# Token sums by column halves, gate products on VectorE, weight sums from tile 11.5, query rows ahead of the gathers

## The chip, the cores and the metric

The kernel runs on one core of a Trainium2 chip. Its engines have their own instruction streams: TensorE (PE) multiplies matrices, VectorE (DVE) and ScalarE (ACT) work elementwise, GpSimd (POOL) does some elementwise work and issues DMA transfers, SyncE (SP) issues most of the transfers. An engine executes its stream in order and waits where an operand isn't there yet. The metric is the device time of one launch in microseconds, as a median of several runs; a profile is one further execution.

## What is computed

One step of a decoder layer, for a prompt of 1024 tokens and 8 sample tokens (1032 columns in all, width 2048). The core of it:

```python
h = rmsnorm(x, norm_w)
(aq, ak, av, iq, ik, iw, az, mq, mk, mv, mi, mf, mo, mz) = split(h @ w_in)
# attention group: an indexer scores all keys, the best 256 are attended to
s     = relu(einsum('bqhd,bld->bqlh', iq, ik))
_, idx = top_k(einsum('bqlh,bqh->bql', s, iw) * IDX_SCALE, 256)
att   = softmax(q @ k[idx] * ATT_SCALE) @ v[idx]
# mLSTM group: chunks of 64 tokens with a carried matrix state C, n, m
h_ml  = mlstm_run(mq, mk, mv, mi, mf)
a     = att * silu(az)
m     = rmsnorm_heads(h_ml) * ml_norm_w * sigmoid(mo) * silu(mz)
y     = rmsnorm(x + concat([a, m]) @ w_out, final_norm_w)
```

For the sample tokens the keys and values are gathered from a paged cache of 4096 past positions, and the mLSTM continues from a given state. Besides `y` the kernel returns the new keys, values, index keys and mLSTM states.

## The kernel before

Everything is float32. A product of two float32 matrices is made of three matmuls of a rounded high part and a low part (`xH`, `xL` for the tokens, `wH`, `wL` for the weights): ACT casts the high part, DVE subtracts it to get the low part.

The input projection runs in 61 tiles of 128 output columns. `proj` (L1500 for its matmuls) makes tile 0 (index keys, indexer weights, gates), tiles 1 to 8 (indexer queries), then `vproj` the eight tiles 9 to 16 of the mLSTM values (L1570, L1575), then tiles 17 to 36: attention keys, values, queries (21 to 28), mLSTM queries (29 to 32) and keys (33 to 36). `evac` (L365 and on) multiplies a finished PSUM bank by the tokens' norm factor (`iqe` at L378, `ev` at L376 and L378) and stores it; the 8 sample columns of a tile are copied into `dec` (L383, L385, and L1595 in `vproj`).

The last 24 tiles (37 to 60: output gates `mo`, SiLU gates `mz` and `az`) are made by `gate_stage` with seven block products in place of eight (L1737). Its operands are sums and differences of blocks. Those of the tokens are made by `job_prep` (L1385): for each of eight pairs of row blocks POOL loads two blocks into one tile `X` (L1391), DVE scales them (L1397) and forms four sums and differences (L1400 to L1404), SP stores five results to `xsD` (L1405, L1406). Those of the weights are made by `job_usum` (L1410): 96 transfers that POOL issues, half of them accumulating (L1416, L1417), each on 512 KB. `gate_stage` runs seven rounds of twelve products; after each product `combine` (L1824) adds a stored partial sum. `half_tanh` (L1762) then makes the gate from a tanh, since sigmoid(x) is (1 + tanh(x/2))/2: ACT's tanh (L1763), then ACT's addition of 1 (L1764). `times` multiplies: tanh plus one by the preactivation (L1788, L1799), then by the partner gate or by the softmax's reciprocal sums (L1789, L1800), on POOL except at the very end, and POOL issues the store to `gateS` (L1790, L1801). The results sit in a ring of four buffers `ev`. `flush` runs the pending `times` in the middle of the next product. A finished row of `gateS` is fetched by POOL (`mixload`, L1466, L1470), multiplied with the attention or mLSTM output by DVE (`mixprod`, L1477, L1478) and split (L1485, L1486); the output projection (L2014, L2081) follows.

The side work (indexer, selection, attention, mLSTM, and for the sample tokens scores, selection, attention and state) is written as generators, called jobs, in three lanes. After each piece of a tile, every lane steps its current job; a job has a first tile, a last tile and a weight, each `yield` names its cost, and the lane spreads the cost over the tiles that are left. A job can also wait for a condition. So the order of instructions interleaves with the projection, and within that a list scheduler orders each engine's stream; `pin` keeps the named instructions in the written order, `tc.high_priority()` moves others ahead. The jobs that matter here, with first and last tile: lane 1 has prep (3 to 10.6), dscore, dsel (9 to 30.5), datt (29 to 37.75, after the index job) and dml; lane 2 has usum (19 to 34).

`job_datt` is the sample tokens' attention. It begins with two gathers of cached keys by POOL (L1283), transposes the sample queries out of `dec` into rows (L1296, then `rows`, L974 to L977, which stores them to `qrowS`), and loads them back broadcast over all partitions (`qload`, L1291). After three pauses it multiplies keys and queries (L1312, pinned) for each sample.

Of the kernel before, what the change touches and what calls it, by code (L numbers as in the profile page):

```python
# [19 lines left out]
NB = 8  # L20
# [151 lines left out]
def body(tc, A, stop=None):  # L172
# [38 lines left out]
    V.memset(mhalf, -0.5)  # L211
    warm = fix.tile([128, 1], F32, name="warm")
    dec = fix.tile([128, T_G, NB], F32, name="dec")
# [99 lines left out]
    def xbegin():  # L313
# [6 lines left out]
        for _, _, load, _ in ws:  # L320
            pin(load(one, SC))
        pin(SC.activation(warm, mhalf, AF.Square))
        for c in range(3):
# [41 lines left out]
    def evac(t, ps, cols, pool=None):  # L365
        full = pool.tile([128, R], F32, name="mfull") if t == T_MISC else None
        chs = chunks(t)
        for c, (c0, cn) in enumerate(chs):
# [13 lines left out]
            if t < T_G and c + 1 == len(chs):  # L382
                G.tensor_copy(dec[:cols, t, :], e[:, cp:cn])  # L383
            if t == T_MISC and c + 1 == len(chs):
                G.tensor_copy(dec[128 - NFILL:, T_MV + 7, :], e[128 - NFILL:, cp:cn])  # L385
            if t == T_MISC:
# [776 lines left out]
    def job_dml():  # L1163
        with tc.tile_pool(name="dm", bufs=1, side="right") as pd:
# [90 lines left out]
            yield 3000  # L1255

    def job_datt():
        with tc.tile_pool(name="da", bufs=1, side="right") as pd:
# [35 lines left out]
            kgs = [gather("ck", b) for b in range(2)]  # L1294
            qc = pd.tile([128, NB, 8], F32, name="ot")
            V.tensor_copy(qc, dec[:, T_AQ:T_AQ + 8, :].rearrange("p j b -> p b j"))  # L1296
            rows(pd, qc.rearrange("p b j -> p (b j)"), qrowS, "jk")
            qbs = [qload(b) for b in range(2)]
            vgs = []
            yield 2500  # L1300
            yield 2500
            yield 2500
            V.tensor_scalar(bias, bias, cc[:, 0:1], NEG, OP.is_ge, OP.mult)
# [81 lines left out]
    def job_prep():  # L1385
        with tc.tile_pool(name="sx", bufs=1, side="right") as px:
            halves = rstd.rearrange("p (h t) -> p h t", h=2)
            for k in range(8):
                X = px.tile([128, 2, 2, HR], F32, name="X")
                for y in (1, 0):  # L1390
                    pin(G.dma_start(X[:, y].rearrange("p h t -> p (h t)"), A["xT"][k + 8 * y]))  # L1391
                    yield 1
                for _ in range(6):
                    yield 1
                a11, a21, a12, a22 = (X[:, y, h] for y in range(2) for h in range(2))
                for y in (1, 0):
                    pin(V.scalar_tensor_tensor(X[:, y], X[:, y], nw[:, k + 8 * y:k + 8 * y + 1], halves, OP.mult, OP.mult))  # L1397
                    yield 1
                O = px.tile([128, 3, HR], F32, name="O")
                pin(V.tensor_tensor(O[:, 0], a21, a22, OP.subtract))  # L1400
                V.tensor_tensor(O[:, 2], a11, a21, OP.subtract)
                yield 1
                pin(V.tensor_tensor(O[:, 1], O[:, 0], a11, OP.subtract))
                V.tensor_tensor(a12, a12, O[:, 1], OP.add)  # L1404
                SY.dma_start(xsD[2:5, k].rearrange("n p t -> p n t"), O)  # L1405
                SY.dma_start(xsD[0:2, k].rearrange("n p t -> p n t"), X[:, 1])  # L1406
                yield 1
                yield 1
# [25 lines left out]
    def ix_weight(blocks):  # L1434
# [9 lines left out]
                   Job("ml", T_G + 8, T_PRE - 0.75, 39, job_ml)]),  # L1444
             Lane([Job("prep", 3, T_MV + 1.6, 8 * 14, job_prep),
                   Job("dscore", T_MV + 1.6, 19.5, 24 + 128 + 2, job_dscore),
                   Job("dsel", T_MV, 30.5, 2000 + 31 * 1700 + 10000 + 16 * 2800 + 2000, job_dsel),
                   Job("datt", T_MQ, T_G + 0.75, 7500 + 8 * 5000 + 34000 + 5 * 2500 + 8000 + 8000 + 5000, job_datt, ix_free),
                   Job("dml", T_G, T_G + 13, 28000 + 16 * 2500 + 5000, job_dml, dml_free)]),
             Lane([Job("usum", 19, T_G - 3, 8 * NP, job_usum)])]  # L1450
    gateV = gateS.rearrange("(k p) r -> k p r", p=128)
# [96 lines left out]
    def vproj():  # L1548
# [5 lines left out]
        for g in range(2):  # L1554
            nv = 512 - g * NFILL
            for (bs, js), span in zip(parts, spans):
# [24 lines left out]
                with tc.high_priority():  # L1581
# [7 lines left out]
                    for p, j in zip(ps[len(bs):], js):  # L1589
                        m = min(128, nv - j * 128)  # L1590
                        for t0, t1 in ((c0, c0 + 256), (c0 + 256, R)):
                            e = evp.tile([128, CN], F32, name="ev")
                            V.tensor_tensor(e[:m, :t1 - t0], p[:m, t0 - c0:t1 - c0], rstd[:m, t0:t1], OP.mult)
                            if t1 == R:
                                G.tensor_copy(dec[:m, T_MV + g * 4 + j, :], e[:m, S - t0:R - t0])  # L1595
                            n = (min(t1, S) - t0) // 128
                            SY.dma_start(mlS[t0 // 128:t0 // 128 + n, :m, g, 4 + j, :].rearrange("c p t -> p c t"),
                                         e[:m, :n * 128].rearrange("p (c t) -> p c t", t=128))
# [38 lines left out]
    def gate_stage():  # L1637
# [124 lines left out]
        def half_tanh(out, e):  # L1762
            SC.activation(out, e, AF.Tanh, scale=0.5)  # L1763
            SC.activation(out, out, AF.Identity, bias=1.0)  # L1764

# [17 lines left out]
        def gate_mz(j, h, e, g):  # L1783
            s2 = ev()
            half_tanh(s2, e)

            def times(eng=G):
                eng.tensor_tensor(s2, s2, e, OP.mult)  # L1788
                eng.tensor_tensor(s2, s2, g, OP.mult)  # L1789
                G.dma_start(row(8 + j)[:, cut(h)], flat(s2))  # L1790
            return times

        def gate_az(j, h, e, g):
# [3 lines left out]

            def times(eng=G):
                eng.tensor_tensor(s2, s2, e, OP.mult)  # L1799
                eng.tensor_tensor(flat(s2)[:, :n], flat(s2)[:, :n], flat(g)[:, :n], OP.mult)  # L1800
                G.dma_start(row(j)[:, cut(h)], flat(s2))  # L1801
# [66 lines left out]
        for i in range(NP):  # L1868
            ps = two()
            product(3, i, 0, ps, True, asker(1, i + 1))  # L1870
            with tc.high_priority():
                put(2, i, combine(ps, got.pop(0), OP.add))
        fill(0, 0)
        ask(2, 0)
        for i in range(NP):
            if i == NM:
                lanes[0].ensure("att")
            ps, g = two(), factor(i, 0, 1)
            product(2, i, 2, ps, True, asker(2, i + 1))
            with tc.high_priority():  # L1880
                f = gate(i, 0, 1, combine(ps, got.pop(0), OP.add), g)
                if f:
                    f()
        for j in late:
# [16 lines left out]
        def last():  # L1901
            flush(V)
            wst.open()
            for q in range(3):
# [4 lines left out]
                first.append((H, L))  # L1909

        for p in range(3):
            fetch(p)
        def push(times, ks=()):
            muls.append((times, ks))

        def flush(eng=G):
            while muls:
                times, ks = muls.pop(0)
                times(eng)
                ready.extend((state["u"], k) for k in ks)  # L1920

        for p, (z, i, y) in enumerate(order):
# [6 lines left out]
            push(f, ks)  # L1929
        flush(V)  # L1930
        for k in pend + [k for _, k in ready]:
# [458 lines left out]
```

## Time and profile before

| | us |
|---|---|
| median of 3 runs | 2028.55 |
| lowest and highest run | 2022.7, 2030.84 |
| the profiled execution | 2028.44 |
| its span, first to last instruction | 2026.6 |
| DVE busy | 1412.7 |
| ACT busy | 929.5 |
| POOL busy | 429.7 |

The mean granted clock of TensorE is 0.98 of full speed. In lines of a timeline the columns are start, duration, engine, line, operation, output and inputs, shapes and count; in brackets stands the idle time of the engine before it and what ended that. In lists by tile the durations are shortest, median and longest in ns, with the first and last start. In lists of waits the columns are total, number of times, and longest.

### The profile page before, as it was taken

How to read it: one execution, taken by the hardware profiler on the slowest of the kernel's cores; microseconds unless marked ns; L12 is line 12 of the kernel's file. 1: busy time of each engine (PE TensorE's matmuls, PEld its weight loads, DVE VectorE, ACT ScalarE, POOL GpSimd, SP SyncE). 2: the span in 40 equal slices, each digit the busy share in tenths (PEclk: the TensorE clock that was granted, in tenths of full speed). 3: DMA queues.
4: the chain of work that ended last, by engine and by line, in shares of the span. 5: the costliest groups of instructions: out<-in, count | busy, mean ns of one | idle time of the engine just before them, and what ended most of it. 6: DMA issues, size and time to landing. Idle time of an engine off the chain costs nothing. (4 is left out here: it accounts for less than half of the span.)

```text
span 2026.6 us, 35929 instructions
## 1 busy us (share of the span) xinstructions
PE 1934.3 (95%) x12710; PEld 1834.8 (91%) x12710; DVE 1412.7 (70%) x3230; ACT 929.5 (46%) x1912; POOL 429.7 (21%) x512
## 2 busy tenths in 40 slices
PE   9996899999999999989999999999999999999997
PEld 9995789999999999989999999999999999977886
DVE  8444568766887968656456667867767556788786
ACT  8111355445413454201256546555765534454555
POOL 0100001112211111143100000002257561107632
PEclk9998899999999999999999999999999999999999
DMA  7476745435776677685733696758788848898875
GB/s 255 123 240 191 203 147 157 138 109 166 209 222 171 182 200 203 166 250 147 231 105 101 191 295 206 238 177 270 229 285 263 214 151 285 263 346 285 275 241 182
DMA packets 252337, 421.30 MB, mean 208 GB/s; under 512 B 39589, under 2 KB 116709, under 8 KB 248317
## 3 DMA queue, kind: packets, MB, share of 16 engines
q1 hardware_dynamic: 234989, 333.08, 52.7%
q0 software_dynamic: 15872, 84.16, 15.1%
q8 instruction: 100, 1.64, 0.3%
q10 hardware_dynamic: 1296, 1.77, 0.2%
q14 instruction: 80, 0.66, 0.1%
HBM read 333.76 MB, written 135.48 MB: 232 GB/s over the span
## 5 line engine op out<-in xcount | busy, mean ns | idle before, releaser
L1500 PE MATMUL pj<-xH,wH 128*128 128x344 f32 (+1 forms) x1200 | 391.1, 329 | 20.4 <-DVE ev L376 7.2
L1500 PE MATMUL pj<-xH,wL 128*128 128x344 f32 (+1 forms) x1200 | 390.6, 326 | 0.8 <-DVE wL L253 0.8
L1500 PE MATMUL pj<-xL,wH 128*128 128x344 f32 (+1 forms) x1200 | 390.7, 326 | 0.2 <-DVE xL L310 0.2
L1737 PE MATMUL pj<-xH 128*128 128x258 f32 x1152 | 330.3, 287 | 6.9 <-ACT mH L1485 6.9
L1737 PE MATMUL pj<-xL,xH 128*128 128x258 f32 x1152 | 330.3, 287 | 0.0
L1737 PE MATMUL pj<-xH,xL 128*128 128x258 f32 x1152 | 329.6, 287 | 0.0
L1500 PEld LDWEIGHTS pj<-xH,wH 128*128 128x128 f32 x1200 | 227.8, 190 | 26.3 <-issue 8.8
L252 ACT CAST wH<-wraw 128x512 fp32r<-128x512 f32 (+2 forms) x183 | 109.8, 609 | 289.9 <-PE pj L1500 128.9
L1500 PEld LDWEIGHTS pj<-xH,wL 128*128 128x128 f32 x1200 | 228.1, 190 | 2.4 <-DVE wL L253 1.2
L1500 PEld LDWEIGHTS pj<-xL,wH 128*128 128x128 f32 x1200 | 228.2, 190 | 2.0 <-DVE xL L310 0.7
L1737 PEld LDWEIGHTS pj<-xH 128*128 128x128 f32 x1152 | 220.4, 191 | 8.4 <-ACT mH L1485 7.2
L1737 PEld LDWEIGHTS pj<-xL,xH 128*128 128x128 f32 x1152 | 220.4, 191 | 0.8
L1737 PEld LDWEIGHTS pj<-xH,xL 128*128 128x128 f32 x1152 | 220.2, 191 | 0.8
L253 DVE TENSOR_TENSOR wL<-wraw,wH 128x512 fp32r<-128x512 f32 (+2 forms) x183 | 126.3, 701 | 79.2 <-ACT wH L252 74.8
L2081 PE MATMUL pj<-wH,sH 128*128 128x512 f32 x336 | 132.2, 394 | 0.6 <-ACT wH L2065 0.4
L2081 PE MATMUL pj<-wH,sL 128*128 128x512 f32 x336 | 131.9, 392 | 0.0
L2081 PE MATMUL pj<-wL,sH 128*128 128x512 f32 x336 | 126.0, 394 | 5.0 <-DVE wL L2070 5.0
L539 ACT ACTIVATE eq<-eq 128x512 bf16<-128x512 bf16 (+2 forms) x93 | 78.4, 843 | 109.0 <-DVE eq L538 109.0
L492 ACT ACTIVATE rl<-bank 128x512 f32<-128x512 f32 (+2 forms) x160 | 80.3, 523 | 87.8 <-PE bank L490 62.7
L495 DVE SCALAR_TENSOR_TENSOR s<-rl,wiN,s 128x512 f32<-128x512 f32 (+2 forms) x150 | 95.3, 655 | 24.8 <-ACT rl L492 22.3
L883 POOL CAST aH<-onec 128x4 fp32r<-128x4 f32 x16 | 4.5, 279 | 399.5 <-DVE onec L822 399.5
L490 PE MATMUL bank<-ki,qi 128*128 128x512 f32 (+2 forms) x320 | 80.6, 358 | 2.8 <-issue 1.9
(508 smaller groups left out, 4747.5 us busy)
## 6 DMA issues: line engine op xcount, KB each, us to landing
usD<-in_wa_dram POOLq DMA_DIRECT2D x72, 512.0 KB
wraw<-in_wt_dram SPq DMA_DIRECT2D x144, 256.0 KB
wraw<-in_wa_dram SPq DMA_DIRECT2D x110, 256.0 KB
wraw<-in_wo_dram SPq DMA_DIRECT2D x64, 256.0 KB
usD<-usD POOLq DMA_DIRECT2D x24, 512.0 KB
xL<-xsD SPq DMA_DIRECT2D x40, 258.0 KB
ev<-spD SPq DMA_DIRECT2D x38, 258.0 KB
spD<-ev SPq DMA_DIRECT2D x36, 258.0 KB
```

The source lines that it names most:

```text
L252: a = SC.copy(H[:, s, :cols], raw[:, s, :cols])
L253: return a, V.tensor_tensor(L[:, s, :cols], raw[:, s, :cols], H[:, s, :cols].bitcast(F32), OP.subtract)
L490: PE.matmul(p[:, :cn], qi[:, h % 4, :], ki[x][:, c0:c0 + cn], start=(x == 0), stop=(x == 1))
L492: SC.activation(r[:, :cn], p[:, :cn], AF.Relu)
L495: v = V.scalar_tensor_tensor(s[:, c0:c0 + cn], r[:, :cn], wv, s[:, c0:c0 + cn], OP.mult, OP.add)
L539: SC.activation(junk2[:, :W1], junk2[:, :W1], AF.Copy, accum_out=cnt[:, 1:2])
L883: G.tensor_copy(aH[:, :, 256:258], onec)
L1500: m = PE.matmul(ps[:cols, :cn], w_[:, k, :cols], x_[kk][:, c0:c0 + cn], start=(kk == ends[0] and z == 0), stop=(kk == ends[1] and z == 2))
L1737: PE.matmul(ps[c], w_[:, q, ks], x[y][:, c * CS:c * CS + CS], start=(first and q == 0 and k == 0 and z == 0), stop=(q == 1 and k == 3 and ...
L2081: PE.matmul(ps[b], S_[x][:, b * 128:b * 128 + 128], T_[y], start=(k == 0 and z == 0), stop=(k == 7 and z == 2))
```

## The change

It has six parts. The copies of sample columns into `dec` go from POOL to DVE. `job_prep` works on quarters of the columns of its two row blocks at a time (columns c to c + 258 of both column halves), in sixteen steps instead of eight, through three `X` buffers, and loads two steps ahead. The query rows become a job of their own, `job_qrows`, ahead of `datt`, which has four pauses in place of three and a last tile of 37.5. `usum` starts at tile 11.5 and ends at 33.5. ACT's addition of 1 goes; `times` is two DVE operations that add the 1 themselves; the products of the fifth round are also flushed in the middle of the next one. The one-element tile `warm` is dropped.

```diff
-    warm = fix.tile([128, 1], F32, name="warm")
...
-        pin(SC.activation(warm, mhalf, AF.Square))
+        pin(SC.activation(rtok[:, 0:1], mhalf, AF.Square))
...
-                G.tensor_copy(dec[:cols, t, :], e[:, cp:cn])
+                V.tensor_copy(dec[:cols, t, :], e[:, cp:cn])
...
+    def job_qrows():
+        with tc.tile_pool(name="qr", bufs=1, side="right") as pd:
+            qc = pd.tile([128, NB, 8], F32, name="qc")
+            V.tensor_copy(qc, dec[:, T_AQ:T_AQ + 8, :].rearrange("p j b -> p b j"))
+            rows(pd, qc.rearrange("p b j -> p (b j)"), qrowS, "jk")
+            yield 1
...
             kgs = [gather("ck", b) for b in range(2)]
-            qc = pd.tile([128, NB, 8], F32, name="ot")
-            V.tensor_copy(qc, dec[:, T_AQ:T_AQ + 8, :].rearrange("p j b -> p b j"))
-            rows(pd, qc.rearrange("p b j -> p (b j)"), qrowS, "jk")
             qbs = [qload(b) for b in range(2)]
             vgs = []
-            yield 2500
-            yield 2500
-            yield 2500
+            for _ in range(4):
+                yield 2500
...
-            for k in range(8):
-                X = px.tile([128, 2, 2, HR], F32, name="X")
+            steps = [(k, c) for k in range(8) for c in range(0, HR, CS)]
+
+            def load(k, c):
+                X = px.tile([128, 2, 2, CS], F32, name="X", bufs=3)
                 for y in (1, 0):
-                    pin(G.dma_start(X[:, y].rearrange("p h t -> p (h t)"), A["xT"][k + 8 * y]))
-                    yield 1
-                for _ in range(6):
-                    yield 1
+                    pin(G.dma_start(X[:, y], A["xT"][k + 8 * y].rearrange("p (h t) -> p h t", h=2)[:, :, c:c + CS]))
+                return X
+
+            Xs = [load(*steps[n]) for n in range(2)]
+            for _ in range(6):
+                yield 1
+            for n, (k, c) in enumerate(steps):
+                X = Xs.pop(0)
+                if n + 2 < len(steps):
+                    Xs.append(load(*steps[n + 2]))
+                yield 1
                 a11, a21, a12, a22 = (X[:, y, h] for y in range(2) for h in range(2))
                 for y in (1, 0):
-                    pin(V.scalar_tensor_tensor(X[:, y], X[:, y], nw[:, k + 8 * y:k + 8 * y + 1], halves, OP.mult, OP.mult))
+                    pin(V.scalar_tensor_tensor(X[:, y], X[:, y], nw[:, k + 8 * y:k + 8 * y + 1],
+                                               halves[:, :, c:c + CS], OP.mult, OP.mult))
                     yield 1
-                O = px.tile([128, 3, HR], F32, name="O")
+                O = px.tile([128, 3, CS], F32, name="O")
...
-                SY.dma_start(xsD[2:5, k].rearrange("n p t -> p n t"), O)
-                SY.dma_start(xsD[0:2, k].rearrange("n p t -> p n t"), X[:, 1])
+                SY.dma_start(xsD[2:5, k, :, c:c + CS].rearrange("n p t -> p n t"), O)
+                SY.dma_start(xsD[0:2, k, :, c:c + CS].rearrange("n p t -> p n t"), X[:, 1])
...
-             Lane([Job("prep", 3, T_MV + 1.6, 8 * 14, job_prep),
+             Lane([Job("prep", 3, T_MV + 1.6, 6 + 16 * 4, job_prep),
...
+                   Job("qrows", T_MQ + 0.5, 31, 1, job_qrows),
-                   Job("datt", T_MQ, T_G + 0.75, 7500 + 8 * 5000 + 34000 + 5 * 2500 + 8000 + 8000 + 5000, job_datt, ix_free),
+                   Job("datt", T_MQ, T_G + 0.5, 10000 + 8 * 5000 + 34000 + 5 * 2500 + 8000 + 8000 + 5000, job_datt, ix_free),
...
-             Lane([Job("usum", 19, T_G - 3, 8 * NP, job_usum)])]
+             Lane([Job("usum", T_MV + 2.5, T_G - 3.5, 8 * NP, job_usum)])]
...
         def half_tanh(out, e):
             SC.activation(out, e, AF.Tanh, scale=0.5)
-            SC.activation(out, out, AF.Identity, bias=1.0)
...
-            def times(eng=G):
-                eng.tensor_tensor(s2, s2, e, OP.mult)
-                eng.tensor_tensor(s2, s2, g, OP.mult)
+            def times():
+                V.scalar_tensor_tensor(s2, s2, 1.0, e, OP.add, OP.mult)
+                V.scalar_tensor_tensor(s2, g, 1.0, s2, OP.add, OP.mult)
                 G.dma_start(row(8 + j)[:, cut(h)], flat(s2))
...
-            def times(eng=G):
-                eng.tensor_tensor(s2, s2, e, OP.mult)
-                eng.tensor_tensor(flat(s2)[:, :n], flat(s2)[:, :n], flat(g)[:, :n], OP.mult)
+            def times():
+                V.scalar_tensor_tensor(s2, s2, 1.0, e, OP.add, OP.mult)
+                V.tensor_tensor(flat(s2)[:, :n], flat(s2)[:, :n], flat(g)[:, :n], OP.mult)
                 G.dma_start(row(j)[:, cut(h)], flat(s2))
...
-            product(2, i, 2, ps, True, asker(2, i + 1))
+            def between(i=i):
+                flush()
+                if i + 1 < NP:
+                    ask(2, i + 1)
+            product(2, i, 2, ps, True, between)
...
-                if f:
-                    f()
+            if f:
+                push(f)
```

More of the change, by code (lines that the diff above doesn't have):

```diff
@@ L382, in evac @@
             if t < T_G and c + 1 == len(chs):
-                G.tensor_copy(dec[:cols, t, :], e[:, cp:cn])
+                V.tensor_copy(dec[:cols, t, :], e[:, cp:cn])
             if t == T_MISC and c + 1 == len(chs):
-                G.tensor_copy(dec[128 - NFILL:, T_MV + 7, :], e[128 - NFILL:, cp:cn])
+                V.tensor_copy(dec[128 - NFILL:, T_MV + 7, :], e[128 - NFILL:, cp:cn])
             if t == T_MISC:
@@ L1387, in job_prep @@
             halves = rstd.rearrange("p (h t) -> p h t", h=2)
-            for k in range(8):
-                X = px.tile([128, 2, 2, HR], F32, name="X")
+            steps = [(k, c) for k in range(8) for c in range(0, HR, CS)]
+            def load(k, c):
+                X = px.tile([128, 2, 2, CS], F32, name="X", bufs=3)
                 for y in (1, 0):
-                    pin(G.dma_start(X[:, y].rearrange("p h t -> p (h t)"), A["xT"][k + 8 * y]))
-                    yield 1
-                for _ in range(6):
-                    yield 1
+                    pin(G.dma_start(X[:, y], A["xT"][k + 8 * y].rearrange("p (h t) -> p h t", h=2)[:, :, c:c + CS]))
[8 more added lines that the diff above has]
+                yield 1
                 a11, a21, a12, a22 = (X[:, y, h] for y in range(2) for h in range(2))
                 for y in (1, 0):
-                    pin(V.scalar_tensor_tensor(X[:, y], X[:, y], nw[:, k + 8 * y:k + 8 * y + 1], halves, OP.mult, OP.mult))
+                    pin(V.scalar_tensor_tensor(X[:, y], X[:, y], nw[:, k + 8 * y:k + 8 * y + 1],
+                                               halves[:, :, c:c + CS], OP.mult, OP.mult))
                     yield 1
-                O = px.tile([128, 3, HR], F32, name="O")
+                O = px.tile([128, 3, CS], F32, name="O")
                 pin(V.tensor_tensor(O[:, 0], a21, a22, OP.subtract))
                 V.tensor_tensor(O[:, 2], a11, a21, OP.subtract)
-                yield 1
-                pin(V.tensor_tensor(O[:, 1], O[:, 0], a11, OP.subtract))
+                V.tensor_tensor(O[:, 1], O[:, 0], a11, OP.subtract)
                 V.tensor_tensor(a12, a12, O[:, 1], OP.add)
-                SY.dma_start(xsD[2:5, k].rearrange("n p t -> p n t"), O)
-                SY.dma_start(xsD[0:2, k].rearrange("n p t -> p n t"), X[:, 1])
-                yield 1
+                SY.dma_start(xsD[2:5, k, :, c:c + CS].rearrange("n p t -> p n t"), O)
+                SY.dma_start(xsD[0:2, k, :, c:c + CS].rearrange("n p t -> p n t"), X[:, 1])
                 yield 1
@@ L1594, in vproj @@
                             if t1 == R:
-                                G.tensor_copy(dec[:m, T_MV + g * 4 + j, :], e[:m, S - t0:R - t0])
+                                V.tensor_copy(dec[:m, T_MV + g * 4 + j, :], e[:m, S - t0:R - t0])
                             n = (min(t1, S) - t0) // 128
@@ L1872, in gate_stage, with push, flush @@
                 put(2, i, combine(ps, got.pop(0), OP.add))
+        def push(times, ks=()):
+            muls.append((times, ks))
+        def flush():
+            while muls:
+                times, ks = muls.pop(0)
+                times()
+                ready.extend((state["u"], k) for k in ks)
         fill(0, 0)
@@ L1901, in last @@
         def last():
-            flush(V)
+            flush()
             wst.open()
@@ L1909, in last @@
                 first.append((H, L))
+        flush()
         for p in range(3):
             fetch(p)
[L1913 to L1920, printed above, removed]
         for p, (z, i, y) in enumerate(order):
@@ L1929, in gate_stage @@
             push(f, ks)
-        flush(V)
+        flush()
         for k in pend + [k for _, k in ready]:
```

## The prediction

> **What bounds the kernel now.** I read the page first, then the windows by stage, then whom TensorE waited for, then the timelines around the longest of those waits.
>
> ```profile
> span 2026.6 us, 35929 instructions
> PE 1934.3 (95%) x12710; PEld 1834.8 (91%) x12710; DVE 1412.7 (70%) x3230; ACT 929.5 (46%) x1912; POOL 429.7 (21%) x512
> ...
> 181.00:260.00 79.00, 56.03 (x241) 47.00 (x240) 39.41 (x63) 22.49 (x44) 3.73 (x7) 0.83 0.64 181
> ...
> 865.00:950.00 85.00, 77.44 (x479) 76.39 (x478) 55.56 (x85) 8.85 (x16) 31.94 (x35) 0.96 0.69 205
> ...
> 1446.00:1600.00 154.00, 146.76 (x1198) 145.27 (x1197) 111.37 (x244) 96.52 (x216) 93.27 (x117) 0.98 0.86 254
> 1600.00:1682.00 82.00, 71.44 (x541) 70.58 (x540) 41.66 (x70) 30.16 (x55) 47.99 (x58) 0.92 0.57 179
> ```
>
> The columns of a window are its length, the busy time of PE, PEld, DVE, ACT and POOL with instruction counts, the granted clock, the DMA share and GB/s. TensorE bounds the kernel: 92.3 us of idle time are all that waits can give back, and its work is not changed. In the four windows it idles 23.0, 7.6, 7.2 and 10.6 us. The next view gives the releasers.
>
> ```profile
> PE pj L1570 <- DVE iqe L378: 15.6, 1, 15.6
> PE pj L1500 <- DVE ev L376: 7.2, 1, 7.2
> PE pj L1500 <- DVE iqe L378: 7.1, 3, 4.4
> PE pj L1737 <- ACT mH L1485: 6.9, 2, 3.8
> PE bank L1570 <- DVE wL L1566: 5.5, 1, 5.5
> ...
> PE pj L1500 <- DVE im L547: 3.8, 1, 3.8
> ...
> POOL X L1391 <- DMA xsD<-X: 76.3, 4, 30.4
> ...
> DVE X L1397 <- DMA X<-in_xT_dram: 49.4, 9, 11.2
> ...
> 207.00:213.00 6.00, 5.38 (x15) 4.52 (x16) 4.38 (x8) 1.49 (x3) 0.59 (x1) 0.56 0.42 99
> ```
>
> The third column is the longest single wait. The six rows of PE hold 46.1 us of the 92.3. The last row is the stretch behind the longest wait: the granted clock is 0.56 there, so 5.38 us of work could have taken about 3.4. I charge 2 us more for every wait of about 4 us or longer.
>
> **The change part by part.** All sums go against the profiled execution: span 2026.6 us, 2028.4 us with what lies around it, beside a median of 2028.55.
>
> A, *token sums by halves*. The two longest waits are one mechanism:
>
> ```profile
> 184.78 1.04 POOL L1391 DMA_DIRECT2D X<-in_xT_dram  x2 [12.60 <-DMA xsD<-X]
> 201.86 1.05 POOL L1391 DMA_DIRECT2D X<-in_xT_dram  x2 [16.04 <-DMA xsD<-X]
> ...
> 188.82 1.29 DVE L1397 SCALAR_TENSOR_TENSOR X<-X,nw,rstd 128x1032 f32<-128x1032 f32 x1 [8.46 <-DMA X<-in_xT_dram]
> ...
> 193.89 0.70 DVE L1404 TENSOR_TENSOR X<-X,O 128x516 f32<-128x516 f32 x1
> 205.80 1.29 DVE L1397 SCALAR_TENSOR_TENSOR X<-X,nw,rstd 128x1032 f32<-128x1032 f32 x1 [11.21 <-DMA X<-in_xT_dram]
> 207.01 0.56 DVE L378 TENSOR_TENSOR iqe<-pj,rstd 128x388 f32<-128x388 f32 x1
> ```
>
> There is one X buffer. DVE finishes it at 194.6, its store has read it at 201.86, only then POOL issues the next load, and DVE, in order, stands at 205.80 with the evacuation that TensorE needs (207.01) queued behind. The round trip is 11.2 us. With three buffers a load is issued two steps ahead. The two k's follow each other in 17 us (184.78 to 201.86), so a half has 8.5 us and a load issued two steps ahead 17, against a round trip of at most those 11.2 for half the bytes. The waits are worth 15.6 + 5.5 + 2 = 23 us. I take 20, since DMA traffic that now moves while TensorE stands still has to move beside it; bounds 10 and 25.
>
> DVE's own work per k goes from 2 x 1.29 + 4 x 0.70 = 5.4 us to 4 operations of 516 columns (0.70 each, the row of that size) and 8 of 258 (0.43, the row at 1671 below) = 6.2: 7 us in all, beside matmuls. Loads and stores double in count, 16 to 32 each. The Trainium skill ("SBUF — State Buffer", The DMA setup-cost knee) says that every transfer pays a fixed 2 us or so, whatever its size, and so speaks against halving. By the trace the row's round trip already holds two such costs; by the page halves save less than half, an estimate of 8 us instead of 5.6 for the round trip, and both hide in 17: the sum is 20 either way. It is a reason for the second rival below.
>
> B, *three shorter waits for iqe before 181 us* (7.1 + 2 = 9 us). They mix waits for X with the gate job's own chain, which stays. I take 4; bounds -2 and 9.
>
> C, *weight sums from tile 11.5, small copies on DVE*.
>
> ```profile
> L1570 PE MATMUL bank<-wH,xH x64: 374/393/628, 181.4 to 422.8; 128*128 128x512 f32 x32, 128*128 128x480 f32 x32
> ...
> L1417 POOL DMA_DIRECT2D usD<-in_wa_dram x48: 767/920/1603, 501.5 to 907.6; - x48
> ...
> 813.39 0.59 POOL L383 COPY dec<-ev 128x8 f32<-128x8 f32 x1 [9.60 <-DVE ev L378]
> 813.92 2.39 POOL L1417 DMA_DIRECT2D usD<-in_wa_dram  x3
> ...
> 830.43 0.62 ACT L252 CAST wH<-wraw 128x512 fp32r<-128x512 f32 x1 [7.84 <-DMA wraw<-in_wa_dram]
> ```
>
> POOL stands at a small copy that waits for DVE; released, it issues 512 KB sums in a burst, three in 2.39 us; the weight load behind them is 7.84 us late, and the 3.8 us wait (im L547) follows. On DVE the copy stands behind its producer and waits for nothing: 37 copies at 0.12 us (the row below) are 4.6 us, behind evacuations. The projection of tiles 9 to 17 runs from 181 to some 425 us, so tile 11.5 is at about 258; the end comes half a tile, some 13 us, earlier than 908. The 96 sums spread from 406 us (4.2 us apart) to about 637 (6.6), so bursts thin out. Worth 3.8 + 2 = 6 us; I take 3 for one burst in two; bounds 0 and 6. The price is F: some 26 sums now fall into the value projection. No row shows them there; the nearest one is a weight load that comes late there already:
>
> ```profile
> 865.50 0.12 DVE L1296 COPY ot<-dec 128x64 f32<-128x64 f32 x1
> ...
> 293.23 0.62 ACT L1565 CAST wH<-wraw 128x512 fp32r<-128x512 f32 x1 [8.35 <-DMA wraw<-in_wv_dram]
> ...
> PE bank L1570 <- ACT wH L1565: 2.4, 1, 2.4
> ```
>
> That cost 2.4 + 2 = 4.4 us. I take two of them, 8 us; bounds 0 and 53 (twelve).
>
> D, *query rows first*.
>
> ```profile
> 870.17 0.47 SPq L977 DMA_DIRECT2D qrowS<-jk  x1
> 876.12 1.30 SPq L1291 DMA_DIRECT2D qb<-qrowS  x3
> ...
> 884.01 1.23 DVE L1312 TENSOR_TENSOR jk<-ck,qb 128x1024 f32<-128x1024 f32 x1 [11.69 <-DMA qb<-qrowS]
> ```
>
> SP waits 6 us for the stored rows, the weight loads wait behind it, and DVE stands 11.7 us; then it works its backlog while TensorE waits 7.2 us for ev L376. Moved are a copy (0.12), a transpose, an evacuation and one store, to where the selection ends; the queries (tiles 21 to 28) are long there. The broadcast loads need no SP wait any more and start with the gathers, about 866, landing some 8 us later (876 to 884 in the rows) at about 874; four pauses instead of three put DVE's first use there too. Worth 7.2 + 2; I take 7; bounds 3 and 9.
>
> E, *gate products on DVE*.
>
> ```profile
> L1764 ACT ACTIVATE ev<-ev x48: 617/636/657, 987.0 to 1674.8; 128x516 f32<-128x516 f32 x48
> ...
> L1788 POOL TENSOR_TENSOR ev<-ev x14: 1286/1300/1572, 1573.9 to 1666.8; 128x516 f32<-128x516 f32 x14
> ...
> 1642.39 3.67 POOL L1789 TENSOR_TENSOR ev<-ev,xL 128x516 f32<-128x516 f32 x2
> ...
> 1643.43 1.50 DVE L1486 TENSOR_TENSOR mL<-mx,mH 128x264 fp32r<-128x264 f32 x1
> 1647.27 0.42 DVE L1486 TENSOR_TENSOR mL<-mx,mH 128x264 fp32r<-128x264 f32 x1
> ...
> 1671.36 0.43 DVE L1824 TENSOR_TENSOR ev<-pj,xH 128x258 f32<-128x258 f32 x1 [3.72 <-POOL ev L1789]
> ```
>
> ACT loses 48 x 0.636 = 30.5 us, off the path. POOL loses 60 products (32 pairs less the last two, which DVE has already). DVE gains 60 x 0.70 = 42 us. In return its operations beside POOL's products get short again: 1.50 against 0.42 us for equal shapes, at most 1.08 for each of the 60 products (1.30 us on POOL), 65 us. DVE's net is between -23 and +42 us over the 236 us of the two windows, where it was busy 153: at most 83%. So it isn't the bound on average. What goes is POOL's time ahead of a free ev buffer: 3.72 us at 1671, and the stretch of 1642 with its 3.8 us wait. The waits of the last window are 10.6 us idle plus 71.4 x 0.08 = 5.7 for the clock, 16 us. I take half, 8, since only the two stretches above lead back to POOL's products. A wait is added, too: the product stands in DVE's order behind ACT's tanh and the gate load, with the combine for TensorE's next banks behind it; POOL bore these waits. The four products of the round before the last, issued at once until now, move to the middle of the next product; nothing reads their rows before the mixing, which hides up to a product's length. Bounds -15 and 16.
>
> ```profile
> L1790 POOL DMA_DIRECT2D gateS<-ev x16: 539/582/636, 1577.0 to 1678.9; - x16
> ```
>
> The gate store stays on POOL: 0.58 us an issue, and the sum is 8. The Trainium skill ("SBUF — State Buffer", A bandwidth-pool intuition that's wrong) has a DMA issued by GpSimd go from 620 to 3100 ns beside a copy on VectorE; that would delay the last stores before the output stage by 2.5 us each, an estimate of 5 us, and make it 3. The rows show no issue over 0.64 us beside a DVE that was 51 to 72% busy in these windows, so I keep 8.
>
> The scratch tile for the first activation is worth nothing: it is written over before its use.
>
> Sum: 20 + 4 + 3 + 7 + 8 - 8 = 34 us, or 2028.4 - 34 = **1994.4**.
>
> **The rivals.**
> - *All covers hold*: 25 + 9 + 6 + 9 + 16 = 65 us, 1963. For it: each wait has a named cause that goes. Against: late loads of other kinds stay.
> - *X stays late*: halves take nearly the time of wholes, and POOL still waits for a store before it loads. A is 5 and B 0: 15 us, 2013. For it: POOL's 76.3 us row. Against: two steps of lead.
> - *DVE takes the bound after 1446 us*: products in order before the combine, E = -15: 11 us, 2017. For it: 72% busy there already. Against: POOL's slowdown goes.
> - *The sums starve the value projection* (slower): 12 of 26 cost 4.4 us each, 53 in place of 8, so 11 us lost: 2039. It decides from ten stalls on, where 42 us of gain are used up. For it: the row at 293. Against: the same sums, closer together, ran beside the projections at 560 to 865 us with few waits.
> - *The change doesn't do what it says*: the instruction order is rebuilt, and pinned work meets other waits: 2028.
>
> **How the numbers follow.** Forecast, 1980 to 2008: 0.50; all covers: 0.10; X late: 0.15; DVE bound: 0.12; starved: 0.08; nothing: 0.05. About 0.5%, 10 us, is what a measurement can tell from no change. Faster takes the first two, 0.12 of the third and 0.08 of the fourth: 0.80; same 0.13; slower 0.07. The range 1976 to 2021 leaves out part of the second case and most of the last two.
>
> **What would show it.** Right: no DVE wait for X over 2 us and no TensorE wait for iqe at L1570; no DVE wait for qb; POOL without products and the 264-column operations all near 0.43 us; DVE up to 83% busy after 1446 us. Wrong: waits of ACT for wraw between 259 and 430 us with TensorE idle behind them; TensorE waiting for the combine after 1446 us; X still loaded late.

## The result and the profile after

The changed kernel is slower: 2048.66 us (median of four runs) against 2028.93 us for the kernel before on the same chip, a ratio of 1.0109 with a 95% interval of 1.0073 to 1.0145. The forecast was 1994.4 us, the range 1976 to 2021. The profiled execution took 2049.09 us, its span is 2047.0 us.

The page of the changed kernel (busy time of each engine; in the slices of 51 us the clock and the DMA share, in tenths):

```profile
span 2047.0 us, 35961 instructions
...
PE 1940.1 (95%) x12710; PEld 1839.2 (90%) x12710; DVE 1429.1 (70%) x3376; ACT 903.8 (44%) x1864; POOL 352.2 (17%) x430
...
PEclk9988999999979999999999999999999999999999
...
DMA  7577757656999222237643478776879977898875
```

POOL lost its products and ACT its additions, as the change says. New is the shape of the DMA line: three slices of 9 (512 to 665 us), and five of 2 or 3 behind them. To see what this costs, I cut both spans into stages by the first and last matmul of each stage's lines (us):

| stage | before | after | difference |
|---|---|---|---|
| up to the value projection | 181.4 | 186.9 | +5.5 |
| value projection | 247.7 | 251.1 | +3.4 |
| tiles 17 to 36 | 536.8 | 568.2 | **+31.4** |
| gate stage | 706.5 | 693.9 | -12.6 |
| first output product | 100.2 | 95.9 | -4.3 |
| second output product and tail | 254.0 | 251.0 | -3.0 |

The loss sits in tiles 17 to 36, where the sum had put a gain of 3 us (C) and 7 (D). The first two rows are not quiet either: a gain and a loss cancel there, as runs 1, 2 and 10 below show. The windows of tiles 17 to 36 (length, busy time of PE, PEld, DVE, ACT and POOL with instruction counts, granted clock, DMA share, GB/s), first before, then after:

```profile
540.00:680.00 140.00, 136.18 (x822) 130.26 (x820) 116.21 (x299) 47.54 (x90) 24.15 (x37) 0.99 0.71 195
680.00:900.00 220.00, 208.71 (x1291) 203.94 (x1291) 161.23 (x407) 79.79 (x144) 47.21 (x69) 0.97 0.71 194
```

```profile
540.00:680.00 140.00, 104.17 (x601) 101.73 (x601) 79.36 (x233) 24.94 (x49) 31.95 (x48) 0.84 0.90 253
680.00:900.00 220.00, 220.00 (x1363) 212.57 (x1362) 185.33 (x482) 105.50 (x191) 0.00 (x0) 1.00 0.23 67
```

Before, the two windows ask the DMA engines for the same share, 0.71. After, the first asks for 0.90 and TensorE idles 35.8 us of 140 there, at a clock of 0.84; in the second the share is 0.23, POOL does nothing for 220 us, and TensorE never idles. Busy time times clock is an estimate of the work done: the two windows hold 136.18 x 0.99 + 208.71 x 0.97 = 337 us of it before and 104.17 x 0.84 + 220.00 = 308 after. By that 30 us are lost, about what the stage is longer.

What TensorE, ACT, DVE and POOL waited for in the changed kernel, over the whole span (total, times, longest):

```profile
POOL ck L1289 <- DVE pb L1269: 265.4, 1, 265.4
...
ACT wH L1576 <- DMA wraw<-in_wv_dram: 40.7, 9, 14.4
...
DVE X L1408 <- DMA X<-in_xT_dram: 20.5, 10, 4.3
...
DVE O L1412 <- DMA xsD<-O: 17.9, 5, 7.4
...
PE pj L1511 <- DVE ev L377: 14.5, 1, 14.5
...
PE bank L1581 <- ACT wH L1576: 13.4, 5, 7.7
...
PE bank L1059 <- DVE cb L1057: 13.1, 2, 8.9
```

In the row of 14.5 us TensorE waits for an evacuation on DVE. It is late because of the operations ahead of it in DVE's order, as the timelines of ACT and DVE show (in brackets the idle time before the instruction and what ended it):

```profile
565.80 0.62 ACT L251 CAST wH<-wraw 128x512 fp32r<-128x512 f32 x1 [22.01 <-DMA wraw<-in_wa_dram]
...
566.45 0.69 DVE L252 TENSOR_TENSOR wL<-wraw,wH 128x512 fp32r<-128x512 f32 x1 [18.89 <-ACT wH L251]
...
571.93 0.51 DVE L377 TENSOR_TENSOR ev<-pj,rstd 128x344 f32<-128x344 f32 x1
```

ACT stood 22 us at its cast for a weight load on SP's queue, DVE 18.89 us behind ACT, and the evacuation came behind that and 5 us of small operations of the index selection. TensorE went on at 572.58. What filled the DMA engines is in POOL's own timeline of the changed kernel:

```profile
547.82 2.24 POOL L1426 DMA_DIRECT2D usD<-usD  x4
560.52 0.81 POOL L1427 DMA_DIRECT2D usD<-in_wa_dram  x1 [10.46 <-DMA usD<-usD]
562.09 0.80 POOL L1427 DMA_DIRECT2D usD<-in_wa_dram  x1 [0.75 <-DMA usD<-usD]
564.27 0.78 POOL L1427 DMA_DIRECT2D usD<-in_wa_dram  x1 [1.38 <-DMA usD<-usD]
...
652.39 0.49 POOL L1426 DMA_DIRECT2D usD<-usD  x1 [2.33 <-DMA usD<-in_wa_dram]
...
918.28 1.04 POOL L1289 DMA_INDIRECT ck<-in_ck_dram,idxs  x1 [265.40 <-DVE pb L1269]
```

POOL issues weight sums of 512 KB one after the other, and each waits for nothing but the landing of an earlier sum. At 652 us all but a few are done, and POOL stands at the next instruction in its order, a gather for the sample tokens' attention, until 918 us. In the kernel before, POOL's timeline of the same stretch has a wait for DVE ahead of each group of sums, at a small copy:

```profile
548.01 0.94 POOL L383 COPY dec<-ev 128x8 f32<-128x8 f32 x1 [14.84 <-DVE im L547]
548.90 2.39 POOL L1417 DMA_DIRECT2D usD<-in_wa_dram  x3
550.44 3.10 POOL L1416 DMA_DIRECT2D usD<-usD  x4
571.88 0.19 POOL L383 COPY dec<-ev 128x8 f32<-128x8 f32 x1 [18.34 <-DVE ev L378]
```

### The profile page after: what moved, and what is told of

Read it like the earlier page. It is cut to its first block, busy times and chain, and to the rows that moved or that the text cites. A ratio compares the mean times of both kernels' runs of the same rounds, so it can differ in the third digit from the quotient of the medians.

```text
span 2047.0 us, 35961 instructions
## 1 busy us (share of the span) xinstructions
PE 1940.1 (95%) x12710; PEld 1839.2 (90%) x12710; DVE 1429.1 (70%) x3376; ACT 903.8 (44%) x1864; POOL 352.2 (17%) x430
## 5 line engine op out<-in xcount | busy, mean ns | idle before, releaser
L1511 PE MATMUL pj<-xH,wH 128*128 128x344 f32 (+1 forms) x1200 | 394.2, 331 | 36.4 <-DVE ev L377 14.5
L1511 PE MATMUL pj<-xL,wH 128*128 128x344 f32 (+1 forms) x1200 | 394.9, 329 | 0.2 <-DVE xL L309 0.2
L2098 PEld LDWEIGHTS pj<-wL,sH 128*128 128x128 f32 x336 | 63.1, 189 | 21.7 <-DVE wL L2087 8.9
```

The lines of the kernel that those rows point to most:

```text
L1511: m = PE.matmul(ps[:cols, :cn], w_[:, k, :cols], x_[kk][:, c0:c0 + cn], start=(kk == ends[0] and z == 0), stop=(kk == ends[1] and z == 2))
L2098: PE.matmul(ps[b], S_[x][:, b * 128:b * 128 + 128], T_[y], start=(k == 0 and z == 0), stop=(k == 7 and z == 2))
```

## The experiments

**My theory** after this reading: the small copies of sample columns, which waited on POOL for each tile's evacuation, were what spaced the weight sums behind them; on DVE they no longer do, and the sums flood the DMA engines. The rivals: the early start of the sums starves the projections, or DVE pays for the copies. All ratios are against the kernel before on the same chip; the chips differ by up to 0.7% in its time, so ratios are compared, not times. A stage time comes from one profiled execution, on whatever chip the run had, so differences of under some 5 us between stages of different runs say nothing. Runs are called by their numbers here.

**1. Copies back on POOL.** The changed kernel with

```diff
-                V.tensor_copy(dec[:cols, t, :], e[:, cp:cn])
+                G.tensor_copy(dec[:cols, t, :], e[:, cp:cn])
```

at all three places.

> Pacing theory: the small copies into dec waited on POOL for each tile's evacuation and so held the weight sums behind them to the projection's pace; on DVE nothing holds them, POOL issues them back to back, and the weight loads starve. With the copies back on POOL the sums should spread from about 285 to 900 us, the 36 us of TensorE idle time between 540 and 680 us go, and the time be about 2005 us (1995 to 2018). Early-start rival: the sums cost what they cost because they start at tile 11.5; then the time stays within 10 us of 2049. DVE rival: the added DVE work delays evacuations; then only the copies' 4.6 us come back, about 2044.

Measured: 0.9932 (0.9905 to 0.9959), tiles 17 to 36 in 529.9 us, and TensorE's idle time from 540 to 680 us is 3.3 us (35.8 in the changed kernel). Three lines are worth 1.8% (1.0109 against 0.9932, 36 us) and turn the loss into a gain.

**2. Sums late again.** The changed kernel, copies on DVE, with

```diff
-             Lane([Job("usum", T_MV + 2.5, T_G - 3.5, 8 * NP, job_usum)])]
+             Lane([Job("usum", 19, T_G - 3, 8 * NP, job_usum)])]
```

> The changed kernel with the sums from tile 19 to 34 as before, copies still on DVE. Pacing theory: in POOL's order all gathers of the index scores now stand ahead of all sums, so some 90 sums run back to back from about 515 us at 2 to 3 us each, at a DMA share near 1 for about 230 us instead of 140; worse than the changed kernel, 2060 to 2110 us, likeliest 2080. Early-start rival: 2010 or less. DVE rival: 2049, no change.

Measured: 1.0108 (1.0062 to 1.0155), tiles 17 to 36 in 574.5 us. The early start isn't the cause: without it the flood is there all the same, a DMA share of 1.01 to 1.04 in each 40 us from 540 to 700 us (packets' times are added up, so a share can pass 1). The size I expected was too large (2060 to 2110 us; 1.0108 of 2029 is 2051). I read it so: the sums are a fixed amount of bytes, and once they are through, TensorE runs without them; from 700 to 740 us the share is 0.20 and TensorE never idles.

**3. Copies alone.** The kernel before with the three copies on DVE and nothing else.

> The kernel before with nothing but the copies moved to DVE. Pacing theory: the same flood of sums from about 515 us on, 2060 to 2110 us, likeliest 2080, and a DMA share near 1 until about 750 us. Early-start rival and DVE rival: 2029 within 6 us, since 37 copies are 4.6 us of DVE time behind evacuations.

Measured: 1.0172 (1.0114 to 1.023), tiles 17 to 36 in 575.4 us. By the ratio that is 2064 us, at the low end of what I expected (2060 to 2110, likeliest 2080), and slower, as the theory says. The two windows of this run:

```profile
540.00:680.00 140.00, 104.14 (x613) 101.35 (x612) 87.32 (x248) 29.85 (x59) 38.38 (x60) 0.87 1.02 287
680.00:900.00 220.00, 216.44 (x1337) 209.34 (x1336) 180.90 (x473) 97.87 (x176) 6.45 (x8) 0.99 0.29 83
```

The same picture as in the changed kernel, with one edit: 35.9 us idle at a DMA share of 1.02, then 0.29.

**4. Copies on both engines.** Runs 1 to 3 can't tell the missing spacing from a price of the copies on DVE. So the changed kernel keeps its copies on DVE, and POOL does the same copy once more behind each:

```diff
                 V.tensor_copy(dec[:cols, t, :], e[:, cp:cn])
+                G.tensor_copy(dec[:cols, t, :], e[:, cp:cn])
```

> The changed kernel with every small copy done on DVE as the change has it, and the same copy done once more on POOL behind it. DVE has all the work that the change gave it, and POOL again waits for each tile's evacuation ahead of the next weight sums. Theory, the copies on POOL had paced the sums: a ratio of 0.990 to 0.996 as with the copies put back on POOL (0.9932), no stretch of 20 us in tiles 17 to 36 with a granted clock under 0.9. Rival, the copies cost on DVE, where they stand ahead of the next evacuations: slower than before as the changed kernel (1.0109), 1.008 to 1.014.

Measured: 0.9911 (0.9893 to 0.9928). Work was added to the changed kernel, and it became 2% faster. POOL's timeline and the first window of this run:

```profile
563.37 0.19 POOL L383 COPY dec<-ev 128x8 f32<-128x8 f32 x1 [21.34 <-DVE im L548]
563.60 0.96 POOL L1428 DMA_DIRECT2D usD<-in_wa_dram  x2
564.56 1.66 POOL L1429 DMA_DIRECT2D usD<-in_wa_dram  x2
582.71 0.72 POOL L383 COPY dec<-ev 128x8 f32<-128x8 f32 x1 [16.49 <-DVE dec L382]
583.38 1.58 POOL L1429 DMA_DIRECT2D usD<-in_wa_dram  x2
584.39 1.70 POOL L1428 DMA_DIRECT2D usD<-usD  x2
607.55 0.57 POOL L383 COPY dec<-ev 128x8 f32<-128x8 f32 x1 [21.46 <-DVE dec L382]
```

```profile
540.00:680.00 140.00, 139.79 (x865) 135.58 (x865) 122.75 (x336) 50.16 (x98) 18.00 (x30) 1.00 0.63 177
```

Four sums, then POOL stands 16 to 21 us at a copy that needs the next tile, then four sums. DVE's copies cost nothing that shows. The idle time on POOL, which looks like waste, is what keeps the weight loads on time: ACT's longest wait for one in this window is 6.5 us, against 22.0 in the changed kernel.

**5. Gate products alone**: the kernel before with the changed `half_tanh`, `times`, `push` and `flush`.

```diff
             SC.activation(out, e, AF.Tanh, scale=0.5)
-            SC.activation(out, out, AF.Identity, bias=1.0)
...
-            def times(eng=G):
-                eng.tensor_tensor(s2, s2, e, OP.mult)
-                eng.tensor_tensor(s2, s2, g, OP.mult)
+            def times():
+                V.scalar_tensor_tensor(s2, s2, 1.0, e, OP.add, OP.mult)
+                V.scalar_tensor_tensor(s2, g, 1.0, s2, OP.add, OP.mult)
```

> The kernel before with the gate products alone on DVE. The changed kernel spends 694.0 us from the first to the last product of the gate stage against 706.6 before and 96.0 against 100.1 in the stage behind it. If that is the products' doing, this gives about 2012 us (2005 to 2018). If it is a later start that lets loads land in time, 2024 to 2032. DVE rival: slower than 2029.

Measured: 0.9909 (0.9879 to 0.9938), gate stage and first output product in 785.2 us, 21.5 less than before. By the ratio that is 2010 us, as expected, and more than twice the gain that the prediction had. The run takes the products, ACT's addition and the later flush together; how the gain divides among them was not measured.

**6. Token sums by halves alone** (the changed `job_prep`, without `warm`).

> The kernel before with the token sums by column halves through three buffers as the only edit. The prediction's terms A and B: 20 us of X waits and 4 us of shorter copies, a ratio of 0.988 (bounds 10 to 25 us: 0.987 to 0.995). Rival, the X waits go (from 49.4 us to about 20 us on DVE) but DVE's time in the stages before the value projection is only moved: the two runs with copies on DVE and late sums, one with the halves and one without, had 417.0 and 422.2 us up to the end of the value projection, so 5 us are gained and the ratio is 0.996 to 1.0, with the bank waits at L1570 down from 15.6 us to under 5 us and iqe waits at the score tiles up to about 10 us.

Measured: 0.9971 (0.9957 to 0.9984), 421.5 us up to the end of the value projection (429.1 before). The rival held: the X waits halve, and the total gains 6 us. Its waits:

```profile
DVE X L1405 <- DMA X<-in_xT_dram: 24.4, 11, 4.0
...
DVE O L1409 <- DMA xsD<-O: 19.5, 5, 7.2
...
DVE O L1410 <- DMA xsD<-O: 9.9, 4, 6.8
```

The waits for X halved (from 49.4 us), and 29.4 us of waits for the result tile `O` came up, which the kernel before doesn't have. `O` has one buffer, and its store has to land before the next step may write it. Ahead of the value projection TensorE now waits 13.4 us for `iqe` (7.1 before), and that stage takes 190.9 us (181.4 before); the value projection itself is 17 us shorter.

**7. Query rows alone** (`job_qrows` and four pauses in `job_datt`).

> The kernel before with the query rows in a job of their own as the only edit. The prediction's term D: 7 us, a ratio of 0.9965; PE's wait of 7.2 us at the query rows gone and tiles 17 to 36 at 530 us. Rival, since the gate products with and without the query rows gave 0.9918 and 0.9909, the wait is replaced by another of the same length: 0.998 to 1.002, tiles 17 to 36 at 534 us or more.

Measured: 1.0035 (1.002 to 1.005): slower, which neither side expected. Tiles 17 to 36 took 529.8 us, but so they did without the query rows (527.9 in run 9, 529.9 in run 11), so that shows no gain of theirs. TensorE's waits between 850 and 960 us in this run:

```profile
PE pj L1504 <- DVE ev L376: 5.0, 1, 5.0
PE pj L1504 <- DVE ev L378: 1.9, 1, 1.9
```

6.9 us where there were 7.2, though DVE waits 3.4 us for the rows in place of 11.7. Where the 0.35% are lost was not found.

**8. Gate products and query rows.**

> The kernel before with the gate products and the query rows of the change, no other edit. The gate products alone gave a ratio of 0.9909 (stages of the gates and of the first output product 785.2 us). The prediction's term D: 7 us more, in tiles 17 to 36 (530 us in place of 536), a ratio of 0.986 to 0.989. Rival, the 7.2 us of PE's wait at the query rows was covered by a wait that now ends last elsewhere: 0.991, tiles 17 to 36 at 536 us.

Measured: 0.9918 (0.9895 to 0.994), beside 0.9909 without the query rows: no gain in the total here either, though tiles 17 to 36 took 530.6 us, as the theory had it.

**9. Early sums alone**: the kernel before with the job's line of run 2 the other way round.

> The kernel before with the weight sums from tile 11.5 in place of 19 as the only edit; the copies stay on POOL. By the pair with the copies on POOL, early (0.9932) and late (0.9888): 4 to 14 us slower, a ratio of 1.002 to 1.007, the value projection 5 to 15 us longer than 247.7 us and tiles 17 to 36 shorter by up to 8 us. Rival, early sums of any kind starve the value projection as the prediction's rival had it: 1.01 or more. Second rival, spreading the sums over more time gains: 0.998 or less, tiles 17 to 36 under 530 us.

Measured: 1.0027 (1.0013 to 1.0042). The value projection took 257.9 us (247.7 before), tiles 17 to 36 527.9. The waits that say why, in this run:

```profile
ACT wH L1565 <- DMA wraw<-in_wv_dram: 29.2, 8, 8.4
...
PE bank L1570 <- ACT wH L1565: 8.3, 3, 3.4
```

Late weight loads do come, as rows of 8.3 us in place of 2.4. The stage is 10 us longer and tiles 17 to 36 are 9 us shorter, so most of it is given back.

**10. Copies and sums both back** (what stays is the halves, the query rows and the gate products).

> The changed kernel with the three small copies on POOL again and the weight sums from their old place (tile 19): what is left of the change is the token sums by halves, the query rows and the gate products. Theory, the early sums starve the value projection: the stages up to the end of the value projection took 435.8 us with sums from tile 11.5 and copies on POOL, and 417.0 us with sums from tile 19; so this run has about 417 us there and tiles 17 to 36 as in the kernel before (530 to 537 us), 1987 us in all, a ratio of 0.980 to 0.986. Rival, the early start costs nothing once the copies pace the sums: 435 us there and 0.993 as with the copies alone put back. Second rival, late sums collide with the gathers of the decode attention and give the gain back in tiles 17 to 36: 417 us in the first stages, but over 545 us there, 0.99 or more.

Measured: 0.9888 (0.9866 to 0.9909), 421.1 us up to the end of the value projection, tiles 17 to 36 in 538.2. Late sums gain 14.7 us there against run 1 and give 8 back, between the theory and its second rival.

**11. Gate products and halves.**

> The kernel before with the gate products and the token sums by halves, no other edit. If the two gains stand beside each other, 0.9909 and 0.9971 make 0.988, about the 0.9888 of the changed kernel with copies and sums both put back, which has the query rows besides. Rival, one covers the other: 0.991 as with the gate products alone.

Measured: **0.984** (0.9815 to 0.9864). This is below both numbers that I had expected (0.988 and 0.991). So neither gain covers the other, and leaving the query rows out gains over run 10 (0.984 against 0.9888).

**12. Two buffers for `O`.** Run 11 with

```diff
-                X = px.tile([128, 2, 2, CS], F32, name="X", bufs=3)
+                X = px.tile([128, 2, 2, CS], F32, name="X", bufs=2)
...
-                O = px.tile([128, 3, CS], F32, name="O")
+                O = px.tile([128, 3, CS], F32, name="O", bufs=2)
```

and a load one step ahead.

> The kernel with the gate products and the token sums by halves, but with two X buffers and two O buffers in place of three and one, and a load issued one step ahead in place of two. With the halves DVE's waits for X fell from 49.4 to 23 us, and in their place it waits 28.6 us for the one O buffer, whose store has to land first (no such wait in the kernel before). Theory, the O buffer took the gain of the halves: the O waits go (under 5 us), the X waits stay under 35 us, the stages up to the end of the value projection take 412 to 418 us in place of 423.9, and the ratio is 0.978 to 0.982 beside 0.984. Rival, one step ahead is too short and the X waits come back to 45 us or more: 0.985 to 0.99. Second rival, DVE's waits there are not what TensorE waits for: O waits gone, but the same 424 us and 0.984.

Measured: 0.9824 (0.9798 to 0.985), 415.9 us up to the end of the value projection (423.9 in run 11). The waits for `O` are gone, and those for X are back:

```profile
DVE X L1405 <- DMA X<-in_xT_dram: 44.2, 11, 7.5
```

The stage gained 8 us as the theory says, the waits for X are as the first rival says, and the two ratios overlap: whether the second buffer pays in the total stays open. Three X beside two O were not tried.

## Why the prediction was wrong

**The step that failed is C**: "On DVE the copy stands behind its producer and waits for nothing", and from it "The 96 sums spread from 406 us (4.2 us apart) to about 637 (6.6), so bursts thin out." The first half is true, and it is why the second isn't. I took the copy's wait on POOL for a defect that makes bursts, and spread the sums by their job's first and last tile. But a place in POOL's order is no time: an instruction that waits for nothing runs when the one ahead of it is done. Behind the last gather of the index scores (515.45 us in the changed kernel, and it waits for TensorE) the copy's wait was the only thing that tied the sums to the progress of the tiles. The row in front of me said so: 9.60 us of POOL at a copy, then three sums. The burst behind that copy cost TensorE 3.8 us where it met a weight load; without the copies' waits the sums cost it some 30 us. Shown by four pairs that differ in the copies: 35 us (1.0172 alone), 36 and 40 (1.0109 against 0.9932 and 0.9911), 45 (1.0108 in run 2 against 0.9888 in run 10). I had put C at a gain of 3 us, with bounds of 0 and 6, on one side only. The runs show that the order of POOL's work holds the sums back only where something in it waits. (DVE's price for the copies was small: 38 copies of 0.17 us, 6.3 us in all, where I had 4.6 from 37 of 0.12, which make 4.4.)

**F**, the price of early sums, was 8 with bounds 0 and 53; alone they cost 0.27%, 5 us, and their waits are the ones named. In the stages up to the end of the value projection the price is larger: they end at 438.0 us in the changed kernel and at 417.0 in run 2, with late sums; at 435.8 and 421.1 in runs 1 and 10. The gain of the halves hides it in the table above. Later stages give part back: in the totals early sums cost nothing (1.0109 against 1.0108) and 9 us (0.9932 against 0.9888). The rival that had the sums starve the value projection forecast 2039, near the measured time, but by luck: most of the starving is in tiles 17 to 36, and its decision point, ten stalls in the value projection, wasn't reached (five waits for `wH`, 13.4 us).

**A and B** were mis-sized: 24 us forecast, 0.29% or 6 us measured. The wait of 15.6 us at L1570 went as described (0.7 us in run 6); the 5.5 us beside it stayed (4.7). B went the other way: the waits for `iqe` ahead of the value projection doubled. The round trip that I put under X belongs to the step as a whole. Its next piece, the one `O` buffer, was in the listing: a load two steps ahead doesn't help a store that must land before the next step writes. The rows of the trace showed no O wait, I think because the X wait came first. The rival that had X late was right in part: POOL still waits 52.1 us for stores before it loads X in run 6 (76.3 before).

**D** was wrong: 7 us forecast, 0.35% lost alone. The row of 7.2 us follows DVE's wait for the query rows in time, but DVE's timeline in run 7, where that wait is down to 3.4 us, has the evacuation behind the same operations:

```profile
868.89 1.22 DVE L1319 TENSOR_REDUCE lT<-jk 128x8 f32<-128x1024 f32 x1
872.85 1.23 DVE L1315 TENSOR_TENSOR jk<-ck,qb 128x1024 f32<-128x1024 f32 x1 [2.74 <-DMA ck<-in_ck_dram,idxs]
874.11 1.22 DVE L1319 TENSOR_REDUCE lT<-jk 128x8 f32<-128x1024 f32 x1
...
877.56 1.22 DVE L1315 TENSOR_TENSOR jk<-ck,qb 128x1024 f32<-128x1024 f32 x1
878.70 0.51 DVE L376 SCALAR_TENSOR_TENSOR ev<-pj,rstd 128x344 f32<-128x344 f32 x1
```

The products and reductions of the attention stand ahead of the evacuation (878.70), and now a gather of the cached keys is part of what they wait for. TensorE waits as long as before. In the changed kernel itself this wait is absent (TensorE's only wait from 850 to 960 us is 2.6 us, for a weight cast), so my sign for step D was fulfilled there and yet proved nothing: POOL's gather stood until 918 us, and the attention came later. One thing stays open. With early sums and query rows TensorE waits 3.4 us between 840 and 985 us in run 1 and 3.0 in run 4, against 8.2 in run 9, early without query rows. Those two runs have the halves and the gate products as well, and no run separates them.

**E** was right in mechanism and undersized: 8 us forecast, 0.91% or 18 us measured, above my upper bound of 16. The two windows of the prediction, in run 11, which has this edit and no flood:

```profile
1446.00:1600.00 154.00, 152.44 (x1281) 152.23 (x1279) 118.07 (x282) 81.89 (x187) 44.43 (x88) 1.00 0.92 279
1600.00:1682.00 82.00, 80.74 (x663) 80.11 (x662) 57.40 (x104) 35.98 (x67) 16.44 (x28) 1.00 0.71 234
```

The idle time there falls from 17.8 us to 2.8 and the clock is back at 1.00. Run 11 is 34 us ahead in its work by then; over the same stretch of work (1412 to 1648 us in it) the idle time is 2.8 us as well. I had taken half of 16 because only two stretches led back to POOL's products; that half was the mis-sized term. DVE's operations that had run beside POOL's products got short, as the rows by tile say: median and longest of the 264-column operation were 434 and 1497 ns before, and in the changed kernel

```profile
L1497 DVE TENSOR_TENSOR mL<-mx,mH x16: 421/426/431, 1633.9 to 1699.3; 128x264 fp32r<-128x264 f32 x16
```

DVE was at most 77% busy in these two windows (118.07 of 154) and 80% over the same stretch of work, so the rival that had it take the bound fell.

The parts add up: -18 (E) - 6 (A, B) + 7 (D) + 5 (F) + 35 (copies) = 23 us, and 20 were measured (2048.66 against 2028.93). That closeness is worth less than it looks: E with A and B make 24 us by these parts and 32 in run 11, so the parts add up only to within some 8 us.

## What to carry to other kernels

Before taking a wait off an engine that issues transfers, ask what stands behind it in that engine's order: a wait can be flow control, and idle time on an engine off the path can be what keeps another's loads on time. When a large stream of transfers is to be spread over a stretch of work, tie it to that work by a dependency, as the copies did here; its place in the program doesn't spread it. A deeper prefetch can just move the wait to the next single buffer of the loop, as in run 6, and a wait that follows another in time need not come from it: undo the cause by itself.

## What the runs showed of the hardware

A stream of large transfers on one queue makes loads on another late. Queues between 540 and 680 us in the changed kernel and in run 4 (packets, MB, and the time of their packets as a share of 16 engines):

```profile
q0 software_dynamic: 2770, 26.25, 69.4%
q1 hardware_dynamic: 7055, 9.11, 20.3%
```

```profile
q0 software_dynamic: 1504, 13.63, 38.1%
q1 hardware_dynamic: 9357, 11.01, 24.9%
```

POOL's sums are in the first queue, SP's weight loads in the second. In the changed kernel a packet of sums takes 0.694 x 16 x 140 / 2770 = 0.56 us of an engine, one of the other queue 0.064 us; in run 4 these are 0.57 and 0.060 us. So the packets do not get slower under the flood. There are more of the long ones, and SP's loads come late: ACT's longest wait for one in the window is 22.0 us, and 6.5 us in run 4. How an engine orders the packets of the two queues, the traces do not show. The Trainium skill ("DMA: Bandwidth & Descriptors", Queues, rings and completion order) says that an engine takes its queues in turn, a packet at a time. No run here shows that order or separates it from a plain lack of bandwidth.
